# TensorE's order in the expert pairs of a two-block transformer, written out and held

## The chip, the cores and the metric

The kernel runs on one core of a Trainium2 chip, as one program. The metric is the time of one execution on the device, in microseconds (us). Five engines work side by side: PE (TensorE, matmuls; PEld is its weight load), DVE (VectorE), ACT (ScalarE), POOL (GpSimd) and SP (SyncE, which here issues the transfers). Transfers come from the chip's memory through one queue, in the order in which SP issues them.

## The reference, cut to what matters

Two blocks of two layers each run over 256 tokens of 1024 numbers, all in float32. The change touches the first block's mixture of experts alone, once in each of its two layers:

```python
xf = h.reshape(T, D)                                  # T 256, D 1024
aff = jax.nn.sigmoid((xf @ router_w).astype(jnp.float32))
...                                                   # 2 of 16 experts for each token, weights w
def expert_block(args):
    xb, e = args
    hid = jax.nn.silu(xb @ w_gate[e]) * (xb @ w_up[e])   # 1024 -> 512
    return hid @ w_down[e]                               # 512 -> 1024
ys = lax.map(expert_block, (xs, blk_expert)).reshape(P, D)
out = jnp.zeros((T, D), ys.dtype).at[tok_buf].add(ys * w_buf[:, None].astype(ys.dtype))
```

The second block (gated feed-forward layers, a recurrent and an attention mixer) follows, in two layers, and is not touched.

## The kernel before, in words

Each layer of the first block has a mixer and then the experts (`moe_body`). There the sixteen experts are worked off in eight pairs `q`, of 64 token slots each. The one-hot matrices `OH[t]` (two tiles of 128 tokens) say which token stands in which slot. For a pair the steps on PE are:

- `gather(b)` (L2039) fetches the tokens of two pairs, 2b and 2b+1, by multiplying the normed tokens with the one-hots, in four quarters of 8 matmuls. Each quarter fills one `bg` bank, which ACT (L2049) and DVE (L2047) empty into `xT`.
- `gateup(q)` (L2073) multiplies `xT` with the gate weights (`w == 0`) and the up weights (`w == 1`), each in two halves `h` of 8 matmuls. The two experts of a pair stand in the two halves of the columns (`i`), so that two matmuls of 64 columns run side by side. The trace counts each of these matmuls as two records: a half is 16 records, a pair's gate and up products 64. ACT makes the silu and DVE the product, `sl`.
- `transOH(q)` (L2054, L2061) transposes the pair's one-hots (`OHT`) and sums the slots' weights (`wsl`).
- `down(q)` transposes `sl` (L187), which ACT copies to `hidT` (L2084), and multiplies with the down weights (L2091, 32 records). DVE scales the result (`yf`), ACT casts its high part (`yh`, L2101), DVE subtracts the rest (`yl`, L2102).
- `combine(q)` (L2111) spreads the slots back over the tokens: for each half `n` of the columns and each token tile two matmuls, with `yh` and `yl`, and DVE adds the sum to `x` (L2113).

Behind pair 4 (`QL` is 5) a loop works off the slots that did not fit into 64: in layer 0 it runs no time, in layer 1 once. `tail()` adds its result, behind the gate and up products of pair 5.

The weights come in tiles of 1024 KB, twelve to a pair (four gate, four up, four down), through a ring of 12 slots (`SLOTS`, L909). `chain` keeps SP's issues in program order, and a load waits until the matmuls that read its slot are done. The next stage's weights stand behind them in the same queue, and their splits into high and low parts (`hi` on ACT L923, `lo` on DVE or POOL L925) come at the layer's end.

Apart from that chain, the order of each engine's instructions is not the program's. The framework's scheduler sets it from a simulated timeline and the data that each instruction needs. Only the last pair's `down` and `combine` have a higher priority.

Of the kernel before, what the change touches and what calls it, by code (L numbers as in the profile page):

```python
# [9 lines left out]
F32 = mybir.dt.float32  # L10
# [837 lines left out]
class Full(Kern):  # L848
# [31 lines left out]
    def block(s):  # L880
        if s.wblock is not s.nc.cur_bb:
            s.wblock, s.wlast, s.wsplit = s.nc.cur_bb, None, deque()

    def chain(s, d):

# [1020 lines left out]
    def moe_body(s, l, end):  # L1906
        nc, I, V, G, A = s.nc, s.I, s.nc.vector, s.nc.gpsimd, s.A
# [3 lines left out]
        hT = [A.tile([128, 4, 256], F32, name="hTf", tag="xT", bufs=3) for j in range(2)]  # L1911
# [17 lines left out]
        for k in range(8):  # L1929
            i = k % 4  # L1930
# [96 lines left out]
        wsl = f("wsl", 8)  # L2027
        xT, OHT = {}, {}

        def gather(b):  # L2030
            for i in range(2):
                xT[2 * b + i] = A.tile([128, 8, 128], F32, name="xT", tag="xT", bufs=3)
            for c in range(0, 8, 2):
                p = s.bg()
                for cc in range(2):
                    first = True
                    for t in range(2):
                        for x in hh[t]:
                            nc.tensor.matmul(p[:, cc * 256:(cc + 1) * 256], x[:, (c + cc) * 128:(c + cc + 1) * 128], OH[t][:, 4 * b:4 * b + 4],  # L2039
                                             start=first, stop=t == 1 and x is hh[t][1])  # L2040
                            first = False
                for cc in range(2):
                    m = s.mT[:, c + cc:c + cc + 1], s.mT[:, 8 + c + cc:9 + c + cc]
                    for i in range(2):
                        o, x = xT[2 * b + i][:, c + cc], p[:, cc * 256 + i * 128:cc * 256 + i * 128 + 128]
                        if i:
                            V.tensor_scalar(o, x, m[0], m[1], op0=OP.mult, op1=OP.add)  # L2047
                        else:
                            nc.scalar.activation(o, x, AF.Identity, bias=m[1], scale=m[0])  # L2049

        def transOH(q):
            p = s.bank("tp", (128, 2, 128))
            for t in range(2):
                nc.tensor.transpose(p[:, t], OH[t][:, 2 * q:2 * q + 2].rearrange("p e s -> p (e s)").bitcast(F32), s.ident)  # L2054
            OHT[q] = A.tile([128, 256], F32R, name="OHT", bufs=2)
            nc.scalar.copy(OHT[q], p.rearrange("p t s -> p (t s)"))
            p = s.bank("tp", (128, 8))
            for i in range(2):
                for t in range(2):
                    e = 2 * q + i  # L2060
                    nc.tensor.matmul(p[64 * i:64 * i + 64, 0:1], OH[t][:, e].bitcast(F32), W[:, t, e:e + 1], start=t == 0, stop=t == 1)  # L2061
            V.tensor_copy(wsl[:, q:q + 1], p[:, 0:1])

        def gateup(q):
            ps = []
            for w in range(2):
                p = s.mm()
                ps.append(p)
                for h in range(2):
                    ws = [s.take() for i in range(2)]  # L2070
                    for k in range(4):
                        for i in range(2):
                            nc.tensor.matmul(p[64 * i:64 * i + 64], xT[q][:, 4 * h + k, 64 * i:64 * i + 64], ws[i][:, k], start=h + k == 0, stop=h + k == 4)  # L2073
            sl = s.a2("sl", (128, 512))
            slv = sl.rearrange("t (k p) -> t k p", k=4)
            ps = [p.rearrange("t (p k) -> t k p", k=4) for p in ps]
            nc.scalar.activation(slv, ps[0], AF.Silu)
            V.tensor_tensor(slv, ps[1], slv, op=OP.mult)
            return sl

        def down(q, hd):
            p = s.trans4(hd)
            hT = s.a2("hidT")
            nc.scalar.copy(hT, p)  # L2084
            ps = [s.bank("m2") for n in range(2)]
            for h in range(2):
                ws = [s.take() for i in range(2)]
                for k in range(2):
                    for n in range(2):
                        for i in range(2):  # L2090
                            nc.tensor.matmul(ps[n][64 * i:64 * i + 64], hT[:, 2 * h + k, 64 * i:64 * i + 64], ws[i][:, k, n * 512:(n + 1) * 512],  # L2091
                                             start=h + k == 0, stop=h + k == 2)
            y = []
            for n in range(2):
                yf = s.a2("yf", (128, 512))
                V.scalar_tensor_tensor(yf, ps[n], wsl[:, q:q + 1], s.mod[5][:, n * 512:(n + 1) * 512], op0=OP.mult, op1=OP.mult)
                yh, yl = (A.tile([128, 512], F32R, name=nm, bufs=2) for nm in ("yh", "yl"))
                if q == 7 and s.YH:
                    V.tensor_copy(yh, yf)
                else:  # L2100
                    nc.scalar.copy(yh, yf)  # L2101
                V.tensor_tensor(yl, yf, yh.bitcast(F32), op=OP.subtract)  # L2102
                y.append((yh, yl))
            return y

        def combine(q, y):
            for n in range(2):
                for t in range(2):
                    p = s.bg()
                    for i in range(2):  # L2110
                        nc.tensor.matmul(p, OHT[q][:, t * 128:(t + 1) * 128], y[n][i], start=i == 0, stop=i == 1)  # L2111
                    xs = s.x[t][:, n * 512:(n + 1) * 512]
                    V.tensor_tensor(xs, p, xs, op=OP.add)  # L2113

# [2 lines left out]
        for q in range(8):  # L2117
            if q == s.QL - 1:
                s.cap = s.CAPL
            if q == s.QL:  # L2120
                combine(q - 1, y)
                y = None
                s.fill()
                tail = s.overflow(l, hh, pos, W, nx, cum)
                s.cap = None
            if q == 7:
                s.ahead.extend(s.nxt)
                if l:
                    s.cap, s.plo = s.ECAP, s.PLO
            hd = gateup(q)  # L2130
            if q == 0:
                for b in range(1, 4):
                    onehot(b)
                counts()
            if q % 2 == 1 and q < 7:
                gather(q // 2 + 1)
            if y is not None:
                combine(q - 1, y)
            if q == s.QL:
                tail()  # L2140
            transOH(q)
            if q == 7:
                with s.tc.high_priority(offset=s.PRI3):
                    y = down(q, hd)
                    combine(q, y)
            else:
                y = down(q, hd)
        for t in range(2):
            end(t)

# [141 lines left out]
```

## Time and profile before

| | |
|---|---|
| time, median of 3 runs | 2462.04 us (2458.93 to 2463.88) |
| the profiled execution's own time | 2461.19 us |
| its span | 2459.4 us |
| PE busy | 94% of the span |
| DVE, ACT, POOL busy | 53%, 42%, 16% |
| share of the DMA engines' time that the weight queue takes | 62% |
| granted TensorE clock, mean | 0.974 of full |

The span is what the trace covers, and the time is some 1.8 us longer. Shares are means over the whole program; the expert stages lie at 252.9 to 504.2 us and at 641.5 to 928.3 us. A wait is put down to the instruction that released it.

### The profile page before, as it was taken

To read this page: it belongs to the slowest core of one execution; us is meant where nothing else is said; L and a number is where in the kernel's file an instruction comes from. 1 tells how busy PE (TensorE), PEld (TensorE's weight loads), DVE (VectorE), ACT (ScalarE), POOL (GpSimd) and SP (SyncE) were. 2 spreads that over 40 slices of the span, in tenths; PEclk is the share of its full clock that TensorE was granted. 3 is DMA by queue.
4 is the path that set the end of the run, shared out by engine and by line. 5 is a ranking of instruction groups with operands and counts; after the bars stand their busy time and mean duration, and the time that the engine had idled before them with its cause. 6 is when DMAs were issued, how large, how long until landed. Compare 5 with 4: busy or idle time off the path is not lost.

```text
span 2459.4 us, 32113 instructions
## 1 busy us (share of the span) xinstructions
PE 2310.1 (94%) x12635; PEld 1635.3 (66%) x12635; DVE 1315.3 (53%) x2121; ACT 1039.4 (42%) x1618; POOL 399.9 (16%) x352
## 2 busy tenths in 40 slices
PE   6999998989899898999888999999999987999999
PEld 4755443366443436888777788887887776788887
DVE  4455322256322226556777756555555877765554
ACT  3454111044210105446655564444444754564543
POOL 1000000010000002002468510000001449620000
PEclk8999999989999898999999999999999998999999
DMA  9676899966798795555433455655655442445552
GB/s 347 242 260 251 334 419 391 413 207 244 308 419 351 312 377 192 188 188 195 138 137 115 140 171 172 197 189 163 205 188 200 166 139 90 138 158 195 171 188 69
DMA packets 240889, 551.33 MB, mean 224 GB/s; under 512 B 11871, under 2 KB 113096, under 8 KB 215392
## 3 DMA queue, kind: packets, MB, share of 16 engines
q1 hardware_dynamic: 240736, 549.26, 62.0%
q8 instruction: 100, 1.64, 0.3%
q14 instruction: 53, 0.43, 0.1%
HBM read 548.15 MB, written 1.06 MB: 223 GB/s over the span
## 4 chain that ended last, share of the span: by engine, by line
PE 61%; DVE 9%; POOL 5%; ACT 2%; issue 2%; DVEq 0%; POOLq 0%; ACTq 0%
PE mm L135 10%; PE mm L137 9%; PE mm L136 9%; PE mm L2073 5%; PE m L135 4%; PE m L136 4%; PE m L137 4%; DVE lo L925 4%; PE m L2091 2%; PE tp L187 2%; PE bg L136 2%; PE bg L135 2%; PE bg L137 2%; POOL rb L605 1%; POOL ra L603 1%
## 5 line engine op out<-in xcount | busy, mean ns | idle before, releaser
L925 DVE TENSOR_TENSOR lo<-w,hi 128x1024 fp32r<-128x1024 f32 (+1 forms) x520 | 659.5, 1308 | 419.9 <-issue 124.0
L923 ACT CAST hi<-w 128x1024 fp32r<-128x1024 f32 (+1 forms) x524 | 519.7, 1040 | 464.5 <-DVE lo L925 352.5
L135 PE MATMUL mm<-hi,hTh 128*128 128x512 f32 (+2 forms) x1200 | 482.5, 404 | 16.5 <-DVE rx L602 8.8
L136 PE MATMUL mm<-lo,hTh 128*128 128x512 f32 (+2 forms) x1200 | 473.7, 395 | 1.0 <-DVE lo L925 1.0
L137 PE MATMUL mm<-hi,hTl 128*128 128x512 f32 (+2 forms) x1200 | 472.0, 394 | 2.1 <-DVE hTl L200 1.9
L135 PEld LDWEIGHTS mm<-hi,hTh 128*128 128x128 f32 x1200 | 229.0, 191 | 65.6 <-DVE rx L602 10.3
L137 PEld LDWEIGHTS mm<-hi,hTl 128*128 128x128 f32 x1200 | 229.0, 191 | 53.0 <-DVE hTl L200 4.2
L2073 PE MATMUL mm<-w,xT 128*64 128x512 f32 x1024 | 258.4, 600 | 3.8 <-issue 2.3
L136 PEld LDWEIGHTS mm<-lo,hTh 128*128 128x128 f32 x1200 | 229.7, 192 | 45.2 <-DVE lo L925 1.8
L2073 PEld LDWEIGHTS mm<-w,xT 128*64 128x64 f32 x1024 | 80.2, 137 | 141.2 <-issue 136.5
L135 PE MATMUL m<-hi,hTh 128*128 128x512 f32 x384 | 156.0, 407 | 9.2 <-DVE rx L602 8.9
L137 PE MATMUL m<-hi,hTl 128*128 128x512 f32 x384 | 153.4, 399 | 0.6 <-DVE hTl L200 0.6
L136 PE MATMUL m<-lo,hTh 128*128 128x512 f32 x384 | 153.7, 400 | 0.0
L2091 PE MATMUL m<-w,hidT 128*64 128x512 f32 x512 | 126.1, 597 | 7.3 <-ACT hidT L2084 6.1
L135 PEld LDWEIGHTS m<-hi,hTh 128*128 128x128 f32 x384 | 74.0, 193 | 26.8 <-DVE rx L602 10.2
L2091 PEld LDWEIGHTS m<-w,hidT 128*64 128x64 f32 x512 | 42.4, 136 | 71.3 <-issue 59.4
L137 PEld LDWEIGHTS m<-hi,hTl 128*128 128x128 f32 x384 | 73.6, 192 | 16.2 <-DVE hTl L200 1.0
L136 PEld LDWEIGHTS m<-lo,hTh 128*128 128x128 f32 x384 | 73.8, 192 | 15.3 <-DVE lo L925 0.8
L212 POOL TENSOR_TENSOR rs<-ss,mhalf 128x1 f32<-128x1 f32 x18 | 10.9, 605 | 428.8 <-DVE ss L210 428.8
L2113 DVE TENSOR_TENSOR x<-bg,x 128x512 f32<-128x512 f32 x64 | 41.8, 686 | 66.2 <-PE bg L2111 66.2
L2049 ACT ACTIVATE xT<-bg,mT 128x128 f32<-128x128 f32 x64 | 28.5, 457 | 113.6 <-PE bg L2039 99.8
L199 ACT CAST hidh<-tp 128x256 fp32r<-128x256 f32 x88 | 32.3, 372 | 101.1 <-PE tp L187 101.0
(612 smaller groups left out, 3467.4 us busy)
## 6 DMA issues: line engine op xcount, KB each, us to landing
w<-in_ffn_w_in_dram SPq DMA_DIRECT2D x176, 512.0 KB, 4.8
w<-in_w_in_dram SPq DMA_DIRECT2D x84, 1024.0 KB, 4.9
w<-in_moe_w_gate_dram SPq DMA_DIRECT2D x64, 1024.0 KB, 10.7
w<-in_moe_w_up_dram SPq DMA_DIRECT2D x64, 1024.0 KB, 12.5
w<-in_moe_w_down_dram SPq DMA_DIRECT2D x64, 1024.0 KB, 11.8
w<-in_ada_w_dram SPq DMA_DIRECT2D x48, 1024.0 KB, 7.4
w<-in_ffn_w_out_dram SPq DMA_DIRECT2D x44, 1024.0 KB, 4.9
w<-in_ev_w_in_dram SPq DMA_DIRECT2D x10, 1024.0 KB, 5.8
```

The costliest lines, as they stand in the source:

```text
L135: nc.tensor.matmul(out, xh, wh, start=first, stop=False)
L136: nc.tensor.matmul(out, xh, wl, start=False, stop=False)
L137: nc.tensor.matmul(out, xl, wh, start=False, stop=last)
L187: s.nc.tensor.transpose(p[:, i], src[:, i * 128:(i + 1) * 128], s.ident)
L199: s.nc.scalar.copy(hi, p)
L603: G.tensor_tensor(a, x, ct[:, t, None, :].to_broadcast([128, 4, 128]), op=OP.mult)
L923: a = s.nc.scalar.copy(hi[:, h], t[:, h]).ins
L925: b = eng.tensor_tensor(lo[:, h], t[:, h], hi[:, h].bitcast(F32), op=OP.subtract).ins
L2049: nc.scalar.activation(o, x, AF.Identity, bias=m[1], scale=m[0])
L2073: nc.tensor.matmul(p[64 * i:64 * i + 64], xT[q][:, 4 * h + k, 64 * i:64 * i + 64], ws[i][:, k], start=h + k == 0, stop=h + k == 4)
L2091: nc.tensor.matmul(ps[n][64 * i:64 * i + 64], hT[:, 2 * h + k, 64 * i:64 * i + 64], ws[i][:, k, n * 512:(n + 1) * 512], start=h + k == 0, ...
L2113: V.tensor_tensor(xs, p, xs, op=OP.add)
```

## The change

A new method `pe()` chains every PE instruction of the pairs to the one before it in the program, by an order that carries no data and no semaphore. So PE keeps the written order, and that order is written anew: `gather(0)` stands whole ahead of pair 0; later gathers come one quarter after `transOH` and one after the `hidT` transposes, over the two pairs ahead of their use; `combine(q-1)` stands in two halves, each behind a half of the next gate product; `hidT` is split out of `down`. At the loop, `combine(4)` stays ahead of it and `tail()` behind `gateup(5)`.

```diff
+    def pe(s, i):
+
+        if s.pblock is not s.nc.cur_bb:
+            s.pblock, s.plast = s.nc.cur_bb, None
+        if s.plast is not None:
+            s.after(i.ins, s.plast)
+        s.plast = i.ins.name
...
-        def gather(b):
+        def gather(b, part=(0, 2, 4, 6)):
             for i in range(2):
-                xT[2 * b + i] = A.tile([128, 8, 128], F32, name="xT", tag="xT", bufs=3)
-            for c in range(0, 8, 2):
+                if part[0] == 0:
+                    xT[2 * b + i] = A.tile([128, 8, 128], F32, name="xT", tag="xT", bufs=3)
+            for c in part:
...
-        def gateup(q):
+        def gateup(q, y):
...
-                            nc.tensor.matmul(p[64 * i:64 * i + 64], xT[q][:, 4 * h + k, 64 * i:64 * i + 64], ws[i][:, k], start=h + k == 0, stop=h + k == 4)
+                            s.pe(nc.tensor.matmul(p[64 * i:64 * i + 64], xT[q][:, 4 * h + k, 64 * i:64 * i + 64], ws[i][:, k], start=h + k == 0, stop=h + k == 4))
+                    if w == 0 and y is not None:
+                        combine(q - 1, y, (h,))
...
-        def down(q, hd):
-            p = s.trans4(hd)
+        def hidT(hd):
+            p = s.bank("tp", (128, 4, 128))
+            for k in range(4):
+                s.pe(nc.tensor.transpose(p[:, k], hd[:, k * 128:(k + 1) * 128], s.ident))
             hT = s.a2("hidT")
             nc.scalar.copy(hT, p)
+            return hT
...
-        def combine(q, y):
-            for n in range(2):
+        def combine(q, y, ns=(0, 1)):
+            for n in ns:
...
-            hd = gateup(q)
+            hd = gateup(q, y)
...
-            if q % 2 == 1 and q < 7:
-                gather(q // 2 + 1)
-            if y is not None:
-                combine(q - 1, y)
             if q == s.QL:
                 tail()
             transOH(q)
+            if q < 6:
+                gather(q // 2 + 1, (4 * (q % 2),))
+            hT = hidT(hd)
+            if q < 6:
+                gather(q // 2 + 1, (4 * (q % 2) + 2,))
             if q == 7:
                 with s.tc.high_priority(offset=s.PRI3):
-                    y = down(q, hd)
+                    y = down(q, hT)
                     combine(q, y)
             else:
-                y = down(q, hd)
+                y = down(q, hT)
```

The order of SP's issues is the same in both kernels. PE's order differs in these places above all. First its gate and up products of pair 0 in layer 0 (`mm_2146` is the gate bank, `mm_2171` the up bank, `bg_2120` and `bg_2133` the third and fourth bank of the gather). Before:

```order
L2073 MATMUL mm_2171<-w_1880,xT_2092 64x512
L2073 MATMUL mm_2171<-w_2052,xT_2092 64x512
L2073 MATMUL mm_2146<-w_1739,xT_2092 64x512
L2073 MATMUL mm_2146<-w_1812,xT_2092 64x512
L2073 MATMUL mm_2171<-w_1880,xT_2092 64x512
L2073 MATMUL mm_2171<-w_2052,xT_2092 64x512
L2039 MATMUL bg_2120<-OH0_2044,hTh0_1989 128x256
L2039 MATMUL bg_2120<-OH0_2044,hTl0_1990 128x256
```

And in the changed kernel:

```order
L2050 MATMUL bg_2133<-OH0_2044,hTh0_1989 128x256
L2050 MATMUL bg_2133<-OH0_2044,hTl0_1990 128x256
L2050 MATMUL bg_2133<-OH1_2045,hTh1_1993 128x256
L2050 MATMUL bg_2133<-OH1_2045,hTl1_1994 128x256
L2085 MATMUL mm_2146<-w_1739,xT_2092 64x512
L2085 MATMUL mm_2146<-w_1812,xT_2092 64x512
L2085 MATMUL mm_2146<-w_1739,xT_2092 64x512
L2085 MATMUL mm_2146<-w_1812,xT_2092 64x512
```

Gate and up took turns, with the last two quarters of the gather between; now the gather is whole ahead of the gate product, and the up product comes behind it.

Second, PE at the end of pair 2's down product in layer 0 and in the gate and up products of pair 3, each row with the number of like ones behind it. Before:

```order
L2091 MATMUL m_2535<-w,hidT 64x512 x2
L2073 MATMUL mm<-w,xT 64x512
L2111 MATMUL bg<-yh,OHT 128x512 x2
L2111 MATMUL bg<-yl,OHT 128x512 x2
L2073 MATMUL mm<-w,xT 64x512 x7
L2111 MATMUL bg<-yh,OHT 128x512
L2111 MATMUL bg<-yl,OHT 128x512
L2111 MATMUL bg<-yh,OHT 128x512
L2111 MATMUL bg<-yl,OHT 128x512
L2073 MATMUL mm<-w,xT 64x512 x24
L187 MATMUL tp<-ident,sl 128x128 x4
```

And in the changed kernel, from the end of pair 0's down product through the gate and up products of pair 1:

```order
L2110 MATMUL m_2563<-w,hidT 64x512 x2
L2085 MATMUL mm<-w,xT 64x512 x8
L2130 MATMUL bg<-yh,OHT 128x512
L2130 MATMUL bg<-yl,OHT 128x512
L2130 MATMUL bg<-yh,OHT 128x512
L2130 MATMUL bg<-yl,OHT 128x512
L2085 MATMUL mm<-w,xT 64x512 x8
L2130 MATMUL bg<-yh,OHT 128x512
L2130 MATMUL bg<-yl,OHT 128x512
L2130 MATMUL bg<-yh,OHT 128x512
L2130 MATMUL bg<-yl,OHT 128x512
L2085 MATMUL mm<-w,xT 64x512 x16
```

The sums of the pair before stood behind the first matmul of the gate product and behind eight; now four stand behind each eight matmuls.

Third, ACT at the end of layer 1's experts, from pair 7's `hidT` on (`hi` belongs to the next weights). Before:

```order
L2084 COPY hidT<-tp 128x512
L2101 CAST yh<-yf 128x512
L923 CAST hi<-w 128x1024
L2101 CAST yh<-yf 128x512
L923 CAST hi<-w 128x1024 x3
```

And in the changed kernel:

```order
L2100 COPY hidT<-tp 128x512
L2120 CAST yh<-yf 128x512
L933 CAST hi<-w 128x1024 x2
L2120 CAST yh<-yf 128x512
L933 CAST hi<-w 128x1024 x2
```

One cast moved from behind the second `yh` to ahead of it.

## Rows read from the trace of the kernel before

**Rows 1.** Windows: us, busy (x) by PE, PEld, DVE, ACT, POOL; clock, DMA, GB/s.

```profile
252.90:401.80 148.90, 141.63 (x686) 58.98 (x686) 42.30 (x88) 25.07 (x50) 3.91 (x6) 1.00 0.93 386
403.80:504.20 100.40, 92.56 (x410) 35.59 (x410) 28.18 (x47) 15.62 (x28) 0.00 (x0) 0.98 0.97 392
641.50:800.00 158.50, 151.45 (x688) 62.12 (x686) 42.26 (x87) 25.47 (x51) 3.91 (x6) 0.99 0.89 363
828.80:928.30 99.50, 91.81 (x410) 36.22 (x410) 27.43 (x44) 16.05 (x28) 4.28 (x2) 0.99 0.98 384
...
280.00:400.00 120.00, 113.54 (x538) 45.27 (x536) 32.48 (x57) 16.87 (x34) 3.06 (x6) 1.00 1.01 419
```

**Rows 2.** PE's waits, 252.9 to 928.3: total us, times, longest.

```profile
PE tp L187 <- DVE sl L2078: 7.9, 9, 0.9
...
PE m L2091 <- ACT hidT L2084: 6.1, 10, 0.7
PE bg L2111 <- DVE x L2113: 5.5, 7, 1.2
PE bg L2111 <- ACT yh L2101: 4.4, 6, 1.0
```

**Rows 3.** Issues at 264.7, 469.3, 766.9: count, KB, us to landing.

```profile
w<-in_moe_w_gate_dram SPq DMA_DIRECT2D x2, 1024.0 KB, 6.9
...
w<-in_moe_w_down_dram SPq DMA_DIRECT2D x1, 1024.0 KB, 13.0
...
w<-in_moe_w_down_dram SPq DMA_DIRECT2D x1, 1024.0 KB, 10.3
```

**Rows 4.** PE timeline, down products and one gate product: start, length.

```profile
490.71 7.14 PE L2091 MATMUL m<-w,hidT 128*64 128x512 f32 x32 [0.73 <-ACT hidT L2084]
...
788.35 7.14 PE L2091 MATMUL m<-w,hidT 128*64 128x512 f32 x32 [0.73 <-ACT hidT L2084]
...
828.84 3.65 PE L2073 MATMUL mm<-w,xT 128*64 128x512 f32 x16 [1.47 <-DVE hk L2257]
...
914.92 7.14 PE L2091 MATMUL m<-w,hidT 128*64 128x512 f32 x32 [0.73 <-ACT hidT L2084]
```

**Rows 5.** PE timeline, gate product of pair 4, layer 0.

```profile
369.28 1.02 PE L2073 MATMUL mm<-w,xT 128*64 128x512 f32 x2
...
372.47 0.47 PE L2111 MATMUL bg<-yh,OHT 128*128 128x512 f32 x1 [0.80 <-DVE x L2113]
...
373.11 3.65 PE L2073 MATMUL mm<-w,xT 128*64 128x512 f32 x14
...
377.35 10.52 PE L2073 MATMUL mm<-w,xT 128*64 128x512 f32 x48
```

**Rows 6.** PE timeline, gate product of pair 2, layer 0.

```profile
316.38 3.65 PE L2073 MATMUL mm<-w,xT 128*64 128x512 f32 x16
319.96 0.50 PE L2111 MATMUL bg<-yh,OHT 128*128 128x512 f32 x1
...
321.09 2.37 PE L2073 MATMUL mm<-w,xT 128*64 128x512 f32 x10
```

**Rows 7.** Busy time of the gather's line alone, one quarter.

```profile
332.80:333.70 0.90, 0.90 (x8) 0.83 (x8) 1.00 0.97 401
```

**Rows 8.** PE and ACT timelines at the start of layer 0's pairs.

```profile
255.78 5.36 PE L2073 MATMUL mm<-w,xT 128*64 128x512 f32 x24
...
256.31 0.81 ACT L2049 ACTIVATE xT<-bg,mT 128x128 f32<-128x128 f32 x2 [1.36 <-DVE xT L2047]
```

**Rows 9.** SP's issues: first of pair 1 in either layer.

```profile
264.27 2.01 SPq L909 DMA_DIRECT2D w<-in_moe_w_gate_dram  x4
...
652.07 4.19 SPq L909 DMA_DIRECT2D w<-in_moe_w_gate_dram  x4
```

**Rows 10.** ACT timeline at the end of layer 0's experts.

```profile
498.39 1.78 ACT L923 CAST hi<-w 128x896 fp32r<-128x896 f32 x2
```

**Rows 11.** PE timeline behind layer 0's overflow loop.

```profile
403.82 5.35 PE L2073 MATMUL mm<-w,xT 128*64 128x512 f32 x16 [2.33 <-issue]
```

More of the change, by code (lines that the diff above doesn't have):

```diff
@@ L882, in block @@
             s.wblock, s.wlast, s.wsplit = s.nc.cur_bb, None, deque()
+    pblock = plast = None
+    def pe(s, i):
[4 more added lines that the diff above has]
+        s.plast = i.ins.name
     def chain(s, d):
@@ L2038, in gather @@
                         for x in hh[t]:
-                            nc.tensor.matmul(p[:, cc * 256:(cc + 1) * 256], x[:, (c + cc) * 128:(c + cc + 1) * 128], OH[t][:, 4 * b:4 * b + 4],
-                                             start=first, stop=t == 1 and x is hh[t][1])
+                            s.pe(nc.tensor.matmul(p[:, cc * 256:(cc + 1) * 256], x[:, (c + cc) * 128:(c + cc + 1) * 128], OH[t][:, 4 * b:4 * b + 4],
+                                                  start=first, stop=t == 1 and x is hh[t][1]))
                             first = False
@@ L2053, in transOH @@
             for t in range(2):
-                nc.tensor.transpose(p[:, t], OH[t][:, 2 * q:2 * q + 2].rearrange("p e s -> p (e s)").bitcast(F32), s.ident)
+                s.pe(nc.tensor.transpose(p[:, t], OH[t][:, 2 * q:2 * q + 2].rearrange("p e s -> p (e s)").bitcast(F32), s.ident))
             OHT[q] = A.tile([128, 256], F32R, name="OHT", bufs=2)
@@ L2060, in transOH @@
                     e = 2 * q + i
-                    nc.tensor.matmul(p[64 * i:64 * i + 64, 0:1], OH[t][:, e].bitcast(F32), W[:, t, e:e + 1], start=t == 0, stop=t == 1)
+                    s.pe(nc.tensor.matmul(p[64 * i:64 * i + 64, 0:1], OH[t][:, e].bitcast(F32), W[:, t, e:e + 1], start=t == 0, stop=t == 1))
             V.tensor_copy(wsl[:, q:q + 1], p[:, 0:1])
-        def gateup(q):
+        def gateup(q, y):
             ps = []
@@ L2079, in gateup, with down @@
             return sl
-        def down(q, hd):
-            p = s.trans4(hd)
+        def hidT(hd):
+            p = s.bank("tp", (128, 4, 128))
+            for k in range(4):
+                s.pe(nc.tensor.transpose(p[:, k], hd[:, k * 128:(k + 1) * 128], s.ident))
             hT = s.a2("hidT")
             nc.scalar.copy(hT, p)
+            return hT
+        def down(q, hT):
             ps = [s.bank("m2") for n in range(2)]
@@ L2090, in down @@
                         for i in range(2):
-                            nc.tensor.matmul(ps[n][64 * i:64 * i + 64], hT[:, 2 * h + k, 64 * i:64 * i + 64], ws[i][:, k, n * 512:(n + 1) * 512],
-                                             start=h + k == 0, stop=h + k == 2)
+                            s.pe(nc.tensor.matmul(ps[n][64 * i:64 * i + 64], hT[:, 2 * h + k, 64 * i:64 * i + 64], ws[i][:, k, n * 512:(n + 1) * 512],
+                                                  start=h + k == 0, stop=h + k == 2))
             y = []
@@ L2110, in combine @@
                     for i in range(2):
-                        nc.tensor.matmul(p, OHT[q][:, t * 128:(t + 1) * 128], y[n][i], start=i == 0, stop=i == 1)
+                        s.pe(nc.tensor.matmul(p, OHT[q][:, t * 128:(t + 1) * 128], y[n][i], start=i == 0, stop=i == 1))
                     xs = s.x[t][:, n * 512:(n + 1) * 512]
```

## Prediction

> **What bounds the kernel now.** The page comes first: by its queues the weights' transfers fill the DMA engines for well under the whole span, so they don't bound the kernel throughout. But the change lies in the two expert stages alone, so I cut these out of the span: per layer the pairs 0 to 4 ahead of the overflow loop and the pairs 5 to 7 behind it, four stretches in all [rows 1]. Two things are to be seen there. PE is idle for the difference of window and busy time: 7.3, 7.8, 7.1 and 7.7 us. And the DMA share is 0.93, 0.97, 0.89 and 0.98, so two limits lie close together. In a stretch where the queue never pauses it moves 419 GB/s [rows 1]; a weight tile of 1024 KB then takes 2.50 us, and the 12 tiles of a pair 30.0 us.
>
> Next I read whom PE waits for. None of the rows names a weight: they name the silu product `sl` (7.9 us), `hidT` (6.1 us), the sum into `x` (5.5 us) and `yh` (4.4 us) [rows 2]. So PE's own order and its neighbours bound the stages now, with the weights a little ahead: the last tile of pair 7 in layer 0 is issued at 469.3 and lands 13.0 us later, at 482.4 [rows 3], and is used in the second half of the products that begin at 490.71 [rows 4], which is 490.71 + 3.45 = 494.2 (half of their 7.14 us, less what the last one overlaps). The lead is 11.8 us. The like for the last tile ahead of layer 1's loop is 767.0 + 10.3 = 777.3 against 788.35 + 3.45 = 791.8 [rows 3, 4], a lead of 14.5 us. A faster PE can gain about these leads, and beyond them only what the queue itself gains.
>
> **What the change moves, on PE.** No matmul is added or removed. It moves the sums of a pair: they stood in twos behind the first two records of the next gate product, and stand now in fours behind 16 whole records; the timeline shows the price of both. Broken order: two records at 369.28, then sums that wait 0.80 us for `x`, 14 records from 373.11, two more sums, the rest of the products from 377.35 [rows 5]; that is 8.07 us. Whole order: 16 records at 316.38, four sums from 319.96, the next records at 321.09 [rows 6]: 3.58 + 1.13 = 4.71 us. In the broken one eight sums stand, which alone cost 2 x 1.13 = 2.26 us, so 16 records cost 5.81 us there, of which 0.80 is the wait; the rest, 5.81 - 3.58 - 0.80 = 1.4 us, is the price of the breaks: half of a 64-column pair of matmuls runs without its partner, and each change between shapes takes about 0.1 us. Such breaks stand in most pairs of both layers.
>
> Here a rule weighs against the change. The Trainium skill (TensorEngine Tiling (Array Packing), Tiling Modes) says that a change of tiling mode drains the TensorE, so that splitting the sums would add drains. The rows bear it out in kind, at about 0.1 us a change, and that is in the 4.71 us already. By the rule at its worst, say twice that (an estimate by this page alone) at four changes a pair in 14 pairs, the gain below would be 5.6 us smaller.
>
> The second part moved is the gather. Its quarter is 8 matmuls in 0.90 us [rows 7], 0.96 us with a change of shape. A quarter now stands between `transOH` and the `hidT` transposes, so PE has about 1.6 us of work while ScalarE and VectorE make `sl`, and the other stands while `hidT` is copied. Both waits, up to 0.9 and 0.7 us [rows 2], are covered for pairs 0 to 5. In pairs 6 and 7 no gather is left: transOH covers only about 0.5 us of `sl`'s wait, and `hidT` stays, 0.35 + 0.73 a pair, 4.3 us over both layers. The sums wait for `yh`, `yl` and `x` no more, because 3.58 us of gate records stand ahead of each half; at the ends (ahead of the loops and behind pair 7) nothing covers them, and some 8 us of the waits in [rows 2] stay there.
>
> The third is `gather(0)`, now whole ahead of the first gate product, which used to begin after two quarters at 255.78 [rows 8]. Its bank is emptied by ScalarE and VectorE in turns (at 256.31 ScalarE ends a wait of 1.36 us for VectorE) [rows 8], some 1.9 us a bank, so PE waits for a bank where it now works. Work moved ahead 1.9 us, new idle 1.6: gate 0 begins at about 259.3, 3.5 us later. In layer 1 I take 2.8 us later, as its start is less crowded.
>
> **The sum.** A pair (1 to 4) on PE after: two blocks of 4.71, up product 6.91, middle 3.2 (transOH 0.6, two quarters 1.92, transposes 0.5, changes of shape 0.2), down product 6.91, together 26.4 us. Pair 0 has no sums: 23.9. Pairs 6 and 7: 25.7, with the waits that stay. Pair 5: 25.6 in layer 0, 28.9 in layer 1 with the overflow tail's 3.3.
> Against it stand the landings: first issue + 2.3 us (a tile issued second lands after 6.9 us, with the first one's 2.5 and its own 2.5 in it [rows 3]) + 2.5 us a tile, and 3.45 us of products behind the last.
>
> - Layer 0 to the loop: PE 259.3 + 23.9 + 4 x 26.4 = 388.8. Weights: the first issue, now 264.27 [rows 9], waits for a slot of gate 0; gate tiles were read k by k with up tiles between, and are now read out after 3.58 us, so about 263.4; with 48 tiles 263.4 + 2.3 + 120 + 3.45 = 389.1.
> - Layer 0's end: the stretch from there to pair 5 stays 6.5 us, so PE would be done at 389.1 + 6.5 + 25.6 + 51.4 = 472.6, the weights at 263.4 + 2.3 + 84 x 2.5 + 3.45 = 479.2. The weights win. Before, the product ends at 490.71 + 7.14 = 497.85 [rows 4]. Gain 18.7.
> - Layer 1 to the loop: PE 648.2 + 23.9 + 105.6 = 777.7; weights, first issue 652.07 [rows 9], here 652.3: + 2.3 + 120 + 3.45 = 778.0. Before 788.35 + 7.14 = 795.5 [rows 4]. Gain 17.5.
> - Layer 1's end, reckoned from the same loop exit: PE 828.84 + 28.9 + 51.4 = 909.1; 30 tiles are issued from the exit on, about 828.84 + 2.3 + 75 + 3.45 = 909.6; for their meeting 910. Before 914.92 + 7.14 = 922.06 [rows 4]. Gain 12.
>
> At the ends the order on ScalarE changes too: in layer 0 two casts `hi` of the next weights (1.78 us for two [rows 10]) now stand ahead of the first `yh` as well, in layer 1 two in place of one ahead of the second, and VectorE's `lo` shift likewise; estimate 1.3 and 1.0 us lost. Sum: 18.7 + 17.5 + 12 - 2.3 = 45.9. That is two limits met exactly. In order, PE stops at each tile that is late, and a slot is freed late then; I take 1.5 us a stretch, 6 in all (about the size of two waits of [rows 2]): **gain 40 us**. The profiled execution's own time is 2461.19, 0.85 under the median of 2462.04; 2461.2 - 40 = **2421 us**.
>
> The bounds. Above: 46 us, 2415. Below: the queue loses what it loses now. In layer 0 the last landing of 482.4 is 5.8 later than 264.27 + 2.3 + 210 = 476.6; ahead of layer 1's loop 777.3 against 774.4, 2.9; behind it I take 4. Then the gain is 45.9 - 12.7 = 33 us, 2428. With jitter on top, 2432.
>
> **Rivals.**
> - Only the named waits go. If breaks cost nothing, the four rows in [rows 2] are all: 23.9 us, of which about 8 at the ends and 4.3 in pairs 6 and 7 stay and 1.6 a layer come in new; 8.4 less the ends' 2.3 leaves 6 us, 2455. For it: what PE's rows name. Against it: the 1.4 us of breaks in [rows 5] against [rows 6], counted without any wait.
> - Weights bound already: the DMA share in [rows 1] is near full and order on PE gives no bytes back; 2459 to 2463. Against it: leads of 11.8 and 14.5 us, and no wait of PE on a weight.
> - Slower. PE held in order can no longer pull other work ahead when a tile is late. After the loop PE stood for 2.33 us, and the first 16 records behind it took 5.35 us [rows 11] where they take 3.65 at the full clock [rows 6]: the granted clock of that stretch is 0.98 [rows 1], so a part of it, by the slow records its start, ran at the lower of the two levels, 1.2 in place of 2.4 GHz. A stand for a weight of that size would cost 2.33 + 1.7 = 4 us. Each layer takes its tiles in 48 pairs, and at a queue of 5.0 us a pair of tiles against 3.5 of products a stand of 1.5 us is possible at each; ten stands of the dear kind eat the gain of 40, from 12 on it is slower; 14 give 2421 + 56 = 2477. Against it: the waits of 0.7 to 0.9 us of today leave records at their usual pace (3.65 us for 14 behind the 0.80 in [rows 5]).
>
> **Chances.** Forecast (2413 to 2432) 0.72; the waits alone (2455) 0.12; weights bound already 0.06; slower 0.05; the rest, 0.05, is a larger gain than the bound or something between 2432 and 2450. For 8 in 10 the range reaches from 2411 towards the first rival: 2411 to 2447. Faster by over 0.2% (5 us, about what the measurement can tell from no change) 0.88, within it 0.07, slower 0.05.
>
> **What would show it.** On PE: blocks of 16 gate records in 3.6 us with four sums behind, no two-record pieces; `sl` and `hidT` waits gone in pairs 0 to 5; a pair of 26 to 30 us instead of 28 to 33. Gate 0 starts later by some 3 us in each layer. The products of pair 7 end near 480 in layer 0, and PE waits for weights there, which it doesn't now. Wrong it would be if PE's idle time grows before the weights by more than the breaks gave, if the granted clock falls in these stretches, or if the time won by the stages is lost again behind them, where the mixer's weights come down the same queue.

## The result, and the profile after

The changed kernel takes 2421.93 us, the median of four runs (2420.70 to 2425.09); the kernel before, run beside it, 2460.55 us (four runs). The ratio is 0.9843 (95% interval 0.9826 to 0.9860), faster by 38.6 us. The forecast was 2421. The profiled execution took 2420.70 us with a span of 2418.9.

The page's first part answers to the 94% of the table (busy us, share, instructions of an engine):

```profile
PE 2274.9 (94%) x12635; PEld 1627.8 (67%) x12635; DVE 1312.8 (54%) x2121; ACT 1041.0 (43%) x1618; POOL 404.9 (17%) x352
```

PE was busy for 2310.1 us before, with the same 12635 instructions. So 35.2 us of the gain are busy time, and only 5.3 us are idle time (149.3 before, 144.0 after, span less busy). Not all of the 35.2 is the change: 4.5 fell ahead of the first gather (223.8 to 219.3 us), where the code is the same. From the first gather to the end of pair 7's down product busy time fell from 230.9 to 219.6 us in layer 0 and from 262.2 to 242.6 in layer 1, together 30.9, and idle time by 8.3. Where the busy time went is seen by line, here PE's gate and up products and its down products over both expert stages (line, count, busy us, mean ns, idle before); the kernel before:

```profile
L2073 PE MATMUL mm<-w,xT 128*64 128x512 f32 x1024 | 258.4, 600 | 3.8 <-issue 2.3 <-DVE hk L2257 1.5
L2091 PE MATMUL m<-w,hidT 128*64 128x512 f32 x512 | 126.1, 597 | 7.3 <-ACT hidT L2084 6.1 <-DVE x L2191 1.1
```

and the changed one:

```profile
L2085 PE MATMUL mm<-w,xT 128*64 128x512 f32 x1024 | 232.5, 599 | 9.3 <-issue 8.0 <-DVE hk L2277 1.3
L2110 PE MATMUL m<-w,hidT 128*64 128x512 f32 x512 | 114.0, 595 | 2.9 <-ACT hidT L2100 2.9
```

Count and mean are the same, but the lines are busy for 25.9 and 12.1 us less. An instruction didn't get shorter; more of them ran beside a partner. The lines of the gather and of the sums, whose instructions are the same, became dearer by 2.9 and 4.4 us. The gate product of pair 1 in layer 0 shows how it now stands on PE (start, length):

```profile
280.65 3.60 PE L2085 MATMUL mm<-w,xT 128*64 128x512 f32 x16
284.18 0.50 PE L2130 MATMUL bg<-yh,OHT 128*128 128x512 f32 x1
...
285.31 3.65 PE L2085 MATMUL mm<-w,xT 128*64 128x512 f32 x16
...
290.02 7.09 PE L2085 MATMUL mm<-w,xT 128*64 128x512 f32 x32
```

Sixteen records, four sums, sixteen records, four sums, 32 records: 280.65 to 285.31 is 4.66 us, to 290.02 another 4.71, as the whole piece of [rows 6]; nothing like the two records of [rows 5] is left. The four stretches (columns as in [rows 1]) are shorter by 7 to 17 us, and PE is idle in them for 2.4, 7.3, 3.2 and 6.2 us:

```profile
249.80:391.80 142.00, 139.57 (x702) 60.89 (x702) 44.28 (x91) 27.31 (x54) 3.92 (x6) 0.99 0.94 387
399.70:490.90 91.20, 83.93 (x394) 31.79 (x394) 27.90 (x44) 14.07 (x24) 0.00 (x0) 0.95 1.00 408
629.50:771.40 141.90, 138.75 (x704) 60.13 (x703) 42.87 (x87) 27.64 (x55) 3.92 (x6) 0.99 0.94 387
800.00:889.00 89.00, 82.79 (x395) 32.35 (x395) 26.43 (x40) 15.00 (x25) 5.13 (x2) 0.99 1.01 402
```

PE's waits, where [rows 2] had sl with 7.9 and hidT with 6.1 us (total, times, longest):

```profile
PE mm L2085 <- issue: 8.0, 1, 8.0
...
PE bg L2130 <- DVE yl L2121: 5.0, 5, 2.2
...
PE bg L2130 <- ACT yh L2120: 3.6, 5, 0.8
...
PE m L2110 <- ACT hidT L2100: 2.9, 4, 0.7
PE bg L2130 <- DVE x L2132: 2.8, 3, 1.7
...
PE tp L2098 <- DVE wsl L2073: 1.1, 4, 0.3
```

`sl` is gone from the list (1.1 us for `wsl` stand in its place in the four pairs without a gather), `hidT` keeps its four waits, in pairs 6 and 7 of both layers, and the sums wait only at the stages' ends. The longest wait is new: 8.0 us ahead of pair 5, behind layer 0's loop, where [rows 11] has 2.33. The chain of waits there names what it is (start, length):

```profile
378.65 20.04 DMA w<-in_moe_w_up_dram
398.69 1.07 issue
399.76 2.82 PE mm L2085 x5
```

PE's last sum ended at 391.8. Up to 398.7 a transfer of the up weights was under way, the last of the six tiles of pair 5 issued ahead of the loop. SP's own waits in 385 to 402 say the same:

```profile
SPq L2216 <- DMA w<-in_moe_w_up_dram: 5.0, 1, 5.0
```

The loop runs no time in layer 0, but its end is a meeting of all engines, and that waits until every tile that was issued has landed. In the kernel before the same meeting ended at 403.8, 1.0 us behind a landing at 402.8, but PE reached it only at 401.5. In the changed kernel and in two of the variants below PE goes on 1.1 us behind the last landing, too.

The stretches side by side, in the two profiled executions, from PE's instructions (us); the forecast's column is worked out from its sum:

| stretch on PE | before | after | gain | forecast |
|---|---|---|---|---|
| start to the first gather of layer 0 | 252.9 | 249.8 | 3.1 | 0 |
| to gate 0 | 2.9 | 6.8 | -3.9 | -3.5 |
| pairs 0 to 4 | 141.5 | 130.9 | 10.6 | 11.7 |
| to pair 5 (loop) | 6.5 | 12.2 | -5.7 | 0 |
| pairs 5 to 7 | 94.0 | 82.6 | 11.4 | 10.4 |
| to the first gather of layer 1 | 143.7 | 146.1 | -2.4 | -1.3 |
| to gate 0 | 3.9 | 7.6 | -3.8 | -2.8 |
| pairs 0 to 4 | 150.1 | 130.9 | 19.2 | 20.3 |
| to pair 5 (loop) | 33.4 | 33.1 | 0.3 | 0 |
| pairs 5 to 7 | 93.2 | 82.2 | 11.0 | 12.0 |
| to the end | 1533.0 | 1532.4 | 0.6 | -1.0 |
| lump for late tiles | | | | -6.0 |
| sum | | | 40.5 | 40 |

The first row is no effect of the change, as PE's order is the same up to there. Half of it arose at two products of 16 records each, which took 3.64 and 3.21 us before, at a granted clock of 0.50 and 0.58, and 1.92 each after, at 1.00; the other half came earlier. In the profiled executions of all kernels here the first gather begins anywhere from 248.1 to 252.9 us. Without this row the rows add up to 37.4 us.

### The profile page after: what moved, and what is told of

Read it like the earlier page. It is cut to its first block, busy times and chain, and to the rows that moved or that the text cites. A ratio compares the mean times of both kernels' runs of the same rounds, so it can differ in the third digit from the quotient of the medians.

```text
span 2418.9 us, 32118 instructions
## 1 busy us (share of the span) xinstructions
PE 2274.9 (94%) x12635; PEld 1627.8 (67%) x12635; DVE 1312.8 (54%) x2121; ACT 1041.0 (43%) x1618; POOL 404.9 (17%) x352
## 4 chain that ended last, share of the span: by engine, by line
PE 73%; DVE 9%; POOL 7%; DMA 3%; ACT 3%; issue 2%; DVEq 0%; SPq 0%; POOLq 0%; ACTq 0%
PE mm L135 10%; PE mm L137 10%; PE mm L136 10%; PE mm L2085 8%; PE m L135 4%; PE m L136 4%; PE m L137 4%; PE m L2110 4%; DVE lo L935 3%; PE tp L187 2%; PE bg L136 2%; PE bg L135 2%; DMA w<-in_moe_w_up_dram 2%; PE bg L137 2%; POOL rb L605 1%
## 5 line engine op out<-in xcount | busy, mean ns | idle before, releaser
L2085 PE MATMUL mm<-w,xT 128*64 128x512 f32 x1024 | 232.5, 599 | 9.3 <-issue 8.0
L2085 PEld LDWEIGHTS mm<-w,xT 128*64 128x64 f32 x1024 | 73.9, 138 | 150.0 <-issue 148.9
L2110 PE MATMUL m<-w,hidT 128*64 128x512 f32 x512 | 114.0, 595 | 2.9 <-ACT hidT L2100 2.9
L135 PEld LDWEIGHTS m<-hi,hTh 128*128 128x128 f32 x384 | 73.9, 192 | 26.2 <-DVE rx L602 9.7
L2110 PEld LDWEIGHTS m<-w,hidT 128*64 128x64 f32 x512 | 36.5, 137 | 69.0 <-issue 62.1
L2115 DVE SCALAR_TENSOR_TENSOR yf<-m,wsl,mod 128x512 f32<-128x512 f32 x32 | 24.0, 751 | 85.3 <-PE m L2110 83.3
```

Source lines behind the costliest of these rows:

```text
L135: nc.tensor.matmul(out, xh, wh, start=first, stop=False)
L2085: s.pe(nc.tensor.matmul(p[64 * i:64 * i + 64], xT[q][:, 4 * h + k, 64 * i:64 * i + 64], ws[i][:, k], start=h + k == 0, stop=h + k == 4))
L2110: s.pe(nc.tensor.matmul(ps[n][64 * i:64 * i + 64], hT[:, 2 * h + k, 64 * i:64 * i + 64], ws[i][:, k, n * 512:(n + 1) * 512], start=h + k = ...
```

## The experiments

**The chain alone left out.** In `pe()`:

```diff
-        if s.plast is not None:
-            s.after(i.ins, s.plast)
         s.plast = i.ins.name
```

> The changed program text, but the chain on PE left out, so that the scheduler sets PE's order again. In PE's order 44 of the 88 uninterrupted pieces of expert products then have an odd number of matmuls, so that one column half runs without its partner; before it is 52 of 95, in the changed kernel 2 of 59. Theory 'breaks': the gain is that pieces are whole; most of it goes, 2445 to 2457 us. Rival 'places': the gain is that the new places of sums and gathers cover the waits for sl and hidT; most of it stays, 2422 to 2432 us.

Measured 2457.38 us (ten runs, 2455.44 to 2458.58), ratio 0.9988 (0.9978 to 0.9998): 0.4 past the end of the theory's range, and the gain is gone. The two lines, as above:

```profile
L2083 PE MATMUL mm<-w,xT 128*64 128x512 f32 x1024 | 252.3, 600 | 3.2 <-DVEq L2214 1.9 <-DVE hk L2275 1.3
L2108 PE MATMUL m<-w,hidT 128*64 128x512 f32 x512 | 125.0, 611 | 7.2 <-ACT hidT L2098 7.2
```

The busy time is back at almost that of before, so the new text without the chain brings next to nothing. Counted row by row in PE's order, 70 of the 768 expert matmuls stand without a partner in this kernel, 72 in the one before, 2 in the changed one.

**The old order, held.** Gathers whole behind odd pairs, sums whole behind the up product:

```diff
-                    if w == 0 and y is not None:
-                        combine(q - 1, y, (h,))
...
+            if q % 2 == 1 and q < 7:
+                gather(q // 2 + 1)
+            if y is not None:
+                combine(q - 1, y)
...
-            if q < 6:
-                gather(q // 2 + 1, (4 * (q % 2),))
             hT = hidT(hd)
-            if q < 6:
-                gather(q // 2 + 1, (4 * (q % 2) + 2,))
```

> The chain kept, but the steps of a pair in the old program's order: gate and up products whole, the gather of two pairs whole behind odd pairs, the eight sums whole, then transOH, hidT and the down products. Theory 'breaks': 8 odd pieces in 38, so the breaks' part of the gain stays; what comes back is the wait for hidT (0.7 us a pair) and about 2.5 us of waiting for a bank in each of the six whole gathers: some 8 + 15 us lost of the 39, 2436 to 2448 us. Rival 'places': the gain goes, 2452 to 2462 us.

Measured 2457.12 us, but spread from 2447.97 to 2460.57. The execution that was profiled is the shortest, 2447.97; its waits:

```profile
PE m L2108 <- ACT hidT L2098: 10.2, 14, 0.7
PE bg L2050 <- DVE xT L2058: 9.5, 8, 1.4
...
PE bg L2128 <- DVE x L2130: 7.4, 16, 1.6
PE bg L2128 <- DVE xT L2058: 5.7, 4, 1.4
```

PE was busy for 2281.2 us there, 28.9 less than before, as the breaks' theory has it; but it waited for 15.7 us more, above all for gather banks that ScalarE and VectorE had not emptied. The profiled execution lies at the upper end of the first theory's range; the median lies outside it, in the rival's. Whole products alone, without the new places of gathers and sums, thus bring little: more than half of the busy time saved comes back as idle time. The longer executions go with a lower granted clock, below.

**Sums whole, gathers in quarters.**

```diff
-                    if w == 0 and y is not None:
-                        combine(q - 1, y, (h,))
...
+            if y is not None:
+                combine(q - 1, y)
```

> The changed kernel, but the eight sums stand whole behind the up product, in place of four behind each half of the gate product. Theory 'breaks': the two places cost the same (four changes of shape a pair become two, 0.2 us a pair less, and the sums help to cover sl in pairs 6 and 7): 2418 to 2424 us. Rival: the sums' place between the gate halves is what gains, since x, yh and yl are waited for elsewhere or the sums delay down: slower than the changed kernel by 5 us or more, 2427 to 2440 us.

Measured 2428.67 us (2427.50 to 2430.19), 6.7 over the changed kernel: the rival, and in part for its reason. PE's busy time is 2272.5, no more than in the changed kernel, but it waits:

```profile
PE bg L2128 <- DVE yl L2119: 9.0, 5, 4.3
PE bg L2128 <- DVE x L2130: 8.7, 15, 2.3
...
PE mm L2085 <- DMA w<-in_moe_w_up_dram: 4.3, 5, 1.3
```

Eight sums in a row wait for VectorE's additions into `x` (8.7 us against 2.8), and the wait for `yl` at layer 1's end is longer (9.0 against 5.0 in all). New are 4.3 us of waits for tiles of the up weights, in pair 4 of both layers and in pair 7 of layer 1. The likely reason, which no run shows: a pair's eight gate and up tiles are now read in one piece and then none for the length of sums and middle, so their slots come free in a bunch. Against all this the stand behind layer 0's loop falls from 8.0 to 5.2 us.

**Gathers whole, sums as changed.**

```diff
-            if q < 6:
-                gather(q // 2 + 1, (4 * (q % 2),))
...
-            if q < 6:
-                gather(q // 2 + 1, (4 * (q % 2) + 2,))
...
+            if q % 2 == 1 and q < 7:
+                gather(q // 2 + 1)
```

> The changed kernel, but each later gather whole behind the up product of an odd pair, in place of quarters on both sides of the hidT transposes. Theory: the waits for sl (about 0.3 us) and hidT (0.7 us) come back in twelve pairs, 12 us, and a whole gather waits for its banks, up to 2.5 us in each of six, 15 us; where weights bound the end of a layer, part of it is hidden: 2432 to 2448 us. Rival: the weights bound all stretches now, so PE has room and nothing changes: 2419 to 2426 us.

Measured 2439.95 us (2438.72 to 2441.49), 18.0 over the changed kernel, in the theory's range. Its waits name the sizes: 11.5 us for banks, 10.2 for `hidT`, 4.5 ahead of the `hidT` transposes, 26.2 together, where the changed kernel has 6.3. Busy time is 4.9 us longer, and the stand behind the loop 6.4 shorter.

```profile
PE bg L2050 <- DVE xT L2058: 11.5, 9, 1.9
PE m L2110 <- ACT hidT L2100: 10.2, 14, 0.7
...
PE tp L2098 <- DVE wsl L2073: 4.5, 15, 0.6
```

**Two quarters of gather(0) behind the first gate half.**

```diff
-        gather(0)
+        gather(0, (0, 2))
...
+                    if q == 0 and w == 0 and h == 1:
+                        gather(0, (4, 6))
```

> The changed kernel, but gather(0) in two halves: two quarters ahead of the first gate half, two behind it. Theory: the first gate product begins 2.5 to 4 us earlier in each layer, its slots come free and the weight stream begins about as much earlier, and since stream and PE are nearly level from there on, most of it reaches the end: 4 to 6 us less than the changed kernel's 2421.9, 2415 to 2418 us. Rival: the start is hidden, as the loop and the layer's end wait for landings that keep their times: 2420 to 2424 us.

Measured 2416.63 us (2415.51 to 2418.95), ratio to the kernel before 0.9823 (0.9807 to 0.9839), 5.3 us under the changed kernel, as the theory has it, and the fastest of all with the whole computation. Gate 0 starts 3.5 us behind the first gather in layer 0 and 3.3 in layer 1, in place of 6.8 and 7.6:

```profile
253.30 3.65 PE L2087 MATMUL mm<-w,xT 128*64 128x512 f32 x16
...
629.81 3.77 PE L2087 MATMUL mm<-w,xT 128*64 128x512 f32 x16
```

But the early start reaches the end in layer 1 alone. In layer 0 the rival holds: both kernels begin their first gather at 249.8, and pair 7's down product ends at 481.7 in place of 482.3. In layer 1 it ends at 878.0 in place of 882.2.

**The last yh on VectorE besides.**

```diff
-    PLO, plo, YH = 15, 0, 0
+    PLO, plo, YH = 15, 0, 1
```

> The same, and the last pair's yh is cast on VectorE in place of ScalarE, where it stood behind the casts of the next weights, which wait for their landing. Theory: both layers' ends get shorter, by 1 to 2 us in layer 0 and about 1 in layer 1: 2 to 3 us under the kernel with gather(0) in halves alone. Rival: VectorE, with its own lo and yl to make, becomes late instead: the same within 1 us, or slower.

Measured 2418.01 us (2415.04 to 2423.12): no gain over the kernel above, the rival. VectorE's timeline at the end of layer 0 shows a reason: the second `yl` stands behind two `lo` of 1.04 us each and ends at 488.9, in the kernel above at 485.8.

```profile
485.88 0.41 DVE L2120 CAST yh<-yf 128x512 fp32r<-128x512 f32 x1
486.21 2.08 DVE L935 TENSOR_TENSOR lo<-w,hi 128x896 fp32r<-128x896 f32 x2
488.22 0.68 DVE L2123 TENSOR_TENSOR yl<-yf,yh 128x512 fp32r<-128x512 f32 x1
```

**Two of twelve tiles a pair left out, in the changed kernel.**

```diff
             for h in range(2):
-                for i in range(2):
+                for i in range(1):
                     out.append((d[e + i].rearrange("(p k) n -> p k n", p=128)[:, 2 * h:2 * h + 2], True))
...
             for h in range(2):
-                ws = [s.take() for i in range(2)]
+                ws = [s.take()] * 2
```

> The changed kernel with two of twelve weight tiles a pair left out (both experts of a pair use the first one's down tiles), so the stream needs 25 us a pair, less than PE's 26.4. Theory: the stand of 8.0 us behind layer 0's loop is the landing of the tiles issued ahead of it and shrinks to 2.5 us or less, and PE's pairs keep their length, since they waited for no weight: 5 to 8 us less than 2421.9, 2413 to 2417 us. Rival 'weights bind all along': pairs get shorter too, 2400 us or less. Rival 'the stand is the loop's own': 2420 to 2424 us.

Measured 2415.78 us (2406.60 to 2418.53). The stand behind the loop is 1.88 us in place of 7.98, as the tiles have landed by then:

```profile
393.06 3.65 PE L2085 MATMUL mm<-w,xT 128*64 128x512 f32 x10 [1.88 <-DVEq L2216]
```

From gate 0 to pair 4's end 130.4 us pass, against 130.9, so in these pairs PE did not wait for weights. Of the 8.0 us 6.1 are the landing of tiles, and 1.9 stay without it.

The time fits the theory, but not by its way. Pairs 5 to 7 did not keep their length: they took 87.2 us in place of 82.6 in layer 0 and 84.9 in place of 82.2 in layer 1. Pair 5's down product, in the changed kernel and in this one:

```profile
423.83 7.09 PE L2110 MATMUL m<-w,hidT 128*64 128x512 f32 x32
...
421.37 7.09 PE L2110 MATMUL m<-w,hidT 128*64 128x512 f32 x32
```

So 2.5 us of the 6.1 are left there. The products of the overflow (`tail()`) are not all in the chain and stand elsewhere here; PE waits 1.6 us for their `yh`, and the granted clock is 0.83 from 410 to 430 us. At the end of layer 1's pair 7 the kernel is ahead by 2.3 us, and 4.3 more come from behind it (1528.1 in place of 1532.4). What the stand alone is worth in time is thus not shown.

**Three tiles ahead of the loop.**

```diff
-    SLOTS, CAP, SPL, DEEP, CAPL = 12, 11, 3, 7, 6
+    SLOTS, CAP, SPL, DEEP, CAPL = 12, 11, 3, 7, 3
```

> The changed kernel with three tiles of pair 5 issued ahead of the loop in place of six. Theory: the loop waits until every tile issued has landed, so the stand falls from 8.0 to 2.5 us or less and pair 5 begins some 5 us earlier in layer 0; but the other tiles are issued behind the loop, and the stream's end moves little, so that most is given back by the end of pair 7: 2418 to 2425 us. Rival 'the gain stays': 2414 to 2417 us. Rival 'the stand is the loop's own': stand of 8 us, 2421 to 2427 us.

Measured 2421.52 us (2416.01 to 2422.98), stand 8.0. The edit did not do what it should: by SP's order six tiles still precede the loop, the last three only issued later, at 385.4 to 389.2. It decides nothing on the theory. Its last tile lands at 399.9, and PE goes on at 401.0.

**A split of one matmul in each gate half, and its control.** With (3, 0) the sums stand behind the seventh of eight matmuls, with (2, 1) behind the sixth:

```diff
-                    if w == 0 and y is not None:
-                        combine(q - 1, y, (h,))
+                            if w == 0 and y is not None and (k, i) == (3, 0):
+                                combine(q - 1, y, (h,))
```

> The changed kernel, but in each gate half the four sums stand one matmul earlier: behind the seventh of eight, so that the last matmul of one column half runs without its partner (24 such splits in both layers, as many changes of shape as in the changed kernel, no new wait). Theory 'breaks': in the profile of before a matmul split off took 0.95 us and the seven behind it as long as eight, so a split costs 0.9 us, 24 of them 21.6; some 5 us of it hide in the stand behind layer 0's loop: 2434 to 2441 us. Rival 'waits': the breaks themselves cost little: 2425 us or less.

> The control to that: the four sums behind the sixth of eight matmuls, so that both column halves stay together and only the place differs. Theory 'breaks': as the changed kernel, 2419 to 2425 us. Rival: any move of the sums off the end of a half costs: as with seven, 2434 us or more.

The control took 2422.43 us, as the changed kernel. The split took 2425.12 (2424.51 to 2426.93): 2.7 us more than the control, by its time at the rival's bound. But the gate and up line shows the breaks' cost, at less than half of my price:

```profile
L2085 PE MATMUL mm<-w,xT 128*64 128x512 f32 x1024 | 241.2, 598 | 6.4 <-issue 5.1 <-DVE hk L2277 1.3
```

That is 8.7 us more than 232.5, or 0.36 us a split. In the timeline of pair 1:

```profile
282.12 3.60 PE L2085 MATMUL mm<-w,xT 128*64 128x512 f32 x14
...
286.77 3.65 PE L2085 MATMUL mm<-w,xT 128*64 128x512 f32 x16
...
291.48 7.94 PE L2085 MATMUL mm<-w,xT 128*64 128x512 f32 x34
```

Seven matmuls (14 records) take 3.60 us, as long as the eight of the changed kernel; the next eight, which begin with the one left over, take no more than eight, because the halves of the columns still alternate across the boundary; and the last piece takes 7.94 us for 17 matmuls in place of 7.09 for 16. So a split costs half of what two partners take together (0.86 us), 0.43, not 0.9. Pair by pair it is the same: from the end of one down product to the next 27.4 us in place of 26.5, for two splits. And of the 8.7 us part is hidden: the stand behind the loop falls from 8.0 to 5.1 us.

**The same two tiles left out of the kernel before.** The edit is the same as in the changed kernel.

> The kernel before with two of twelve weight tiles a pair left out (both experts use the first one's down tiles). Theory: no weight was waited for, PE's order bound it: 2454 to 2462 us. Rival 'weights bound already': the stages fall towards 25 us a pair: 2440 us or less.

Measured 2425.32 us (2423.26 to 2428.85): 35.6 us faster, where the theory said no change. But it doesn't show a bound by weights either. The scheduler had a shorter stream to reckon with and set another order on PE: matmuls left over of the gate product stand beside such of the down product (PE's timeline):

```profile
333.50 0.64 PE L2073 MATMUL mm<-w,xT 128*64 128x512 f32 x1
333.51 0.64 PE L2091 MATMUL m<-w,hidT 128*64 128x512 f32 x1
333.98 0.59 PE L2073 MATMUL mm<-w,xT 128*64 128x512 f32 x1
333.99 7.02 PE L2091 MATMUL m<-w,hidT 128*64 128x512 f32 x30
```

At 333.50 and 333.51 two of different products run side by side, and so at 333.98 and 333.99. The waits for `sl` are gone and those for `hidT` fall from 6.1 to 0.7 us. From the first gather to the end of pair 7's down product PE's idle time fell in the two layers together from 32.4 to 12.0 us, its busy time only from 493.1 to 484.6. So here most of the gain is waits; the changed kernel removed 8.3 us of them. Stream and order changed together, so this run can't part them; whether the weights alone would have let the old order go faster stays open.

**The old order, held, again.**

> A second look at the old order held on PE, whose times lie between 2448 and 2461 us with a mean granted clock from 0.973 down to 0.966. Theory: its whole gathers let PE stand 1.4 us twice each, and in the long executions the clock is at the lower level behind such stands: if this one takes 2455 us or more, the granted clock of the expert stretches is below 0.98 where the first look had 0.99 to 1.00, with waits of the same length. Rival: the waits themselves are longer, at the same clock. If it takes about 2448 us, it tells nothing.

It took 2448.76 us with a clock of 0.973, at the short end again, and so it tells nothing of the long executions.

## Why the prediction held, point by point

- *The order is the price, not the named waits.* Right, and the main point: in the pairs of both layers 30.9 us of busy time went, and idle time fell by 8.3, near the 6 us that the rival of the waits alone would have had. The chain is needed for it (2457.38 without). But it is not enough: the old order held has 28.9 us less busy time than the kernel before and takes 2448 to 2461 us, as PE then waits longer. The forecast's second part, the gather in quarters, is needed as well.
- *1.4 us for the broken product of pair 4.* The sum fits, the reading was too dear for one break: the two pieces of [rows 5] are two matmuls without a partner, 0.43 each, and changes of shape. 70 such matmuls fewer, at 0.43, are 30 us, an estimate. The two lines of the expert products lost 38.0; the other 8 us were not taken apart, but the products also lie in fewer pieces (95 before, 59 after).
- *The Trainium skill's drain at a change of tiling mode* cost no more than in the sum: the changed kernel keeps four changes for the sums of a pair, in 12 pairs and not in 14 as the prediction counts, and takes 4.71 us a block. The Trainium skill (TensorEngine Tiling (Array Packing), Key Properties) also says that different tiles can work in parallel; this case's traces agree, and show the other side, that half the array stands idle when the order separates partners.
- *sl and hidT covered by quarters.* Right: with whole gathers the three waits come to 26.2 us where they are 6.3, and 18.0 us of time are back. The 4.3 us forecast for pairs 6 and 7 are 2.9 + 1.1.
- *A pair at 26.4 us.* Right: pair 1 takes 280.65 to 307.2, 26.5. Pairs 0 to 4 took 130.9 us in both layers, forecast 129.8.
- *gather(0) costs 3.5 and 2.8 us.* Measured 3.9 and 3.8, but only 0.8 and 1.4 of that are waits for a bank; the granted clock at these gathers is 0.75 and 0.76, after PE's idle time ahead of them. In the kernel before it was 1.00 and 0.73 there, so in layer 1 the low clock is not new.
- *Layer 0 ends at 479.2, bound by weights.* Neither the step nor the size held. The product ends at 482.3, of which 3.1 us are the first row of the table; counted from the first gather layer 0 gained 12.4 us where 18.7 were forecast. The sign that was named, PE waiting for weights there, did not come: it waited for a weight in no pair; the last tile landed at 478.3 and was used at 478.7, so PE and stream came out level. What failed is "the stretch from there to pair 5 stays 6.5 us": it is 12.2, because the faster PE met the landing of six tiles. The stream also paused there as before, from the last landing to the first issue behind the loop, which the lower bound of the forecast had (5.8 us) and its middle had not.
- *6 us of jitter, and the total.* Its size was right and its cause was not: in place of small stands at late tiles it was the loop's 5.7 us in layer 0, and from there to the end of layer 1's pairs the gain fell short too (24.3 us where 28.2 were forecast). The rows that the change made add up to 37.4 us; that the profiled time came within 1 us of the forecast took the 3.1 us ahead of the first gather, and that is luck.
- *The layers' ends.* Right in kind: ScalarE's casts of the next weights wait for their landing and `yh` stands behind them; and VectorE's `lo`, which follow these casts, stand between the two `yf` and ahead of `yl`,

```profile
480.80 1.78 ACT L933 CAST hi<-w 128x896 fp32r<-128x896 f32 x2 [5.59 <-DMA w<-in_od_w_in_dram]
482.48 0.61 ACT L2120 CAST yh<-yf 128x512 fp32r<-128x512 f32 x1
...
482.43 1.09 DVE L935 TENSOR_TENSOR lo<-w,hi 128x896 fp32r<-128x896 f32 x1
483.44 0.74 DVE L2115 SCALAR_TENSOR_TENSOR yf<-m,wsl,mod 128x512 f32<-128x512 f32 x1
...
485.10 1.29 DVE L2121 TENSOR_TENSOR yl<-yf,yh 128x512 fp32r<-128x512 f32 x2
```

but 2.4 us were lost to layer 1's first gather where 1.3 were forecast, and after layer 1 nothing that can be told apart.

## What to carry to other kernels

Where products run as partners in the two halves of the array's columns, count in the order of TensorE's queue how many stand without a partner: they look busy, no wait names them, and here they held some 30 us of busy time, by count and price. Busy time saved is not yet time saved: 24 splits added 8.7 us to the line and 2.7 us to the kernel, and with products made whole, but no new places for the work between them, more than half of the busy time saved came back as waits. Before a product is sped up, ask where the next meeting point of all engines is and what it waits for: here a loop that runs no time let PE stand for 8.0 us once PE came to it early. And try the work between products in pieces: the same sums in one block instead of two cost 6.7 us.

## What the runs showed of the hardware

The old order held on PE took between 2448 and 2461 us in ten runs with one program, and its time goes with the mean granted clock:

```
time us   2447.97 2450.06 2451.62 2453.38 2456.49 2457.75 2459.37 2460.50 2460.50 2460.57
clock       0.973   0.971   0.971   0.969   0.968   0.967   0.967   0.967   0.966   0.966
```

The kernel before has 0.973 to 0.975 in the runs beside it. Both profiled executions of this order are at the short end, so where the clock fell in the others was not seen. That its stands of 1.4 us for a bank do it is argued, not shown: the kernel with gathers whole has such stands too (up to 1.9 us), and its clock stays at 0.973 to 0.974. In the changed kernel the cost of a long stand is seen in two windows (columns as in [rows 1]):

```profile
391.80:399.70 7.90, 0.00 (x0) 0.00 (x0) 0.76 (x2) 0.00 (x0) 0.00 (x0) 0.58 0.69 281
399.70:412.00 12.30, 12.24 (x50) 4.00 (x52) 0.00 (x0) 0.60 (x1) 0.00 (x0) 0.85 0.92 371
```

While PE stands the granted clock is 0.58 of full on the mean, near the lower of its two levels (1.2 and 2.4 GHz); in the 12.3 us behind it is 0.85, and the 48 gate and up records there take 12.28 us where 10.52 are usual [rows 5]. So the stand of 8.0 us cost another 1.8. That is no new cost: the kernel before lost 1.7 us behind its stand of 2.33 (16 records in 5.35 us for 3.65, [rows 11]), and the kernel with splits as much behind 5.07 (48 in 12.21).
